# Pair-wide stacks, stores from GpSimd's queue and a scaling on ScalarE in a two-layer encoder on one NeuronCore

## The chip, the core and the metric

The kernel runs on one core of one Trainium2 chip. A core has five engines that run their own instruction streams: TensorE (PE, with its weight load shown apart as PEld), VectorE (DVE), ScalarE (ACT), GpSimd (POOL) and SyncE (SP, which here only issues DMAs). DMAs are issued by SP, ACT and POOL; the profile calls the issuing sides SPq, ACTq and POOLq. The metric is the device time of one execution in microseconds (us). A change of 0.5% is about 12 us.

## What is computed

The reference is a two-layer bidirectional encoder on a sequence of 512 tokens of width 1024, in float32. Each layer is a half-step SwiGLU feed-forward part, a mixer, and another half-step feed-forward part, each between two RMS norms. The change touches the mixer and the projection in front of it:

```python
u = rmsnorm(h, mix_pre_g[l])
proj = u @ w_in[l]
qa, ka, va, qb, kb, vb, qc, kc, vc, gl = jnp.split(proj, split_at, axis=-1)
oa = neighbourhood_attention(...)   # A: 8 heads of 64, 2-D window and bias
ob = sliding_window_attention(...)  # B: 8 query heads, 2 key heads, rotary, sink
# C: 4 heads, two maps each, rotary
sc = jnp.einsum('bhtqd,bhtkd->bhtqk', qblk, k).astype(jnp.float32) * (d ** -0.5)
p = jax.nn.softmax(sc, axis=-1)
a = p[:, :, 0] - lam * p[:, :, 1]
o = jnp.einsum('bhqk,bhke->bhqe', a.astype(v.dtype), v)
...
merged = jnp.sum(gates * yb, axis=2)   # yb: three branches through w_branch
h = h + rmsnorm(merged @ w_out[l], mix_post_g[l])
```

## The kernel before

Every matrix product is made from parts: a float32 value x is split into `hi`, a rounded copy that ACT writes, and `lo`, the rest x - hi, that DVE writes (`split`, lines 348 to 357). A dense product is then three matmuls, hi by hi, hi by lo and lo by hi (lines 326 to 328 for one output block, 680 in the projection's faster scheme). The weights are fetched in pieces of 512 KB (line 211) by SP or by ACT, and split by ACT (L224) and DVE (L225) on the way to PE.

For attention the parts are stacked instead. A head has 64 channels, so a tile of 128 partitions holds `hi` of a head in one half and `lo` in the other. A product of a stack of q with the stack of k sums hi by hi and lo by lo, a second one with the swapped stack of k (lo on top of hi) sums the cross terms. Each stack is filled by two DMAs, one for each half. The output channels of the projection come in blocks of 128, which are two heads: a *pair*.

*The projection* (profile time 350 to 508 us in the first layer, 1540 to 1707 in the second) makes all blocks of q, k, v. `stacked` (L1414) splits a block; those of pair 0 of branch A are stacked at once into the tiles `early`, all others are stored to memory as `part` by `store` (L1403, its DMA is L1405, issued by SP): `hi` and `lo` are separate regions there. `turned` transposes v and stores its two parts, or keeps them for pair 0. q and k of branch C are stored as they are, as `raw`.

*The mixer* (508 to 860, 1707 to 2060) runs a list of units, ORDER (line 72): `qa`, `qb`, `qc` bring in a pair or head, `aa`, `ab`, `ac` are the attentions, `ga` to `gc` are gate products, `ya` to `yc` the branches' products with w_branch. The list says in which order the work is written; a scheduler then places each engine's instructions, so that PE does gate and branch products (L326 to L328) between the pieces of attention. The units around the change:

- `restacked` (L1753) brings a pair's stacks back: for each head one stack of q, and for k the stack and the swapped stack. Each half is a DMA of SP (L1762, L1763, the tile `st`). With q of a pair and k of a pair these are 12 DMAs of 128 KB.
- `values` loads v's two parts, as two DMAs (`load`, L1739). The bias rows (L1712, `braw`) and the masks (L1706) are loads of SP as well.
- `softmax_pv` is the attention of A and B: products with k and swapped k (L1659), softmax, and in `rest` the transposes (L1690) and products with v (L1693, L1694).
- `attn_c` is the attention of branch C. For each of the four blocks of 128 queries of a head, and each of two maps: products (L1843, L1844), the maximum on DVE (L1845, L1846), the exponential on ACT (L1850). Then DVE takes the reciprocal of both sums (L1854), scales the second map by its reciprocal and by minus lambda (L1855), and adds the scaled first map (L1858). In `rest` PE transposes the result (L1867) and multiplies with v (L1870 to L1872); DVE copies the output out of PSUM (L1874), ACT squares it (L1877).
- `qkv_c` loads q and k of a head of branch C from `raw`, turns them by the rotary tables on DVE (L1748 to L1750), splits them and stacks them with DMAs between tiles (`stacks`, L1625).
- `combine` multiplies a branch, takes the gate (`gate`), which for branches B and C comes back from memory into the tiles `gd`, and adds to `merged` with GpSimd (L1916). At the end `merged` is split into M (L1970).

SP issues its DMAs in the order of its own list: an issue that waits holds all that stand behind it.

## Time and profile before

| | |
|---|---|
| median of three runs | 2406.46 us (2402.06 to 2411.33) |
| the profiled execution | 2405.37 us |
| its span on the core | 2403.6 us |
| mean granted clock of TensorE | 0.994 |

The span is the time from the first to the last instruction in the trace; 1.8 us of the execution's time lie around it. Busy times of matmuls are modelled ends in a pipeline, so rows of PE can overlap and be longer than the distance from one start to the next. "PE x <- DVE y" in a list of waits says that PE stood idle until an instruction of DVE, at the line named, had ended. The columns of a window's row are its limits, its length, the busy time and number of instructions of each engine, the clock that TensorE was granted (1 is full speed), the share of the 16 DMA engines that was busy, and GB/s.

### The profile page before, as it was taken

To read this page: it belongs to the slowest core of one execution; us is meant where nothing else is said; L and a number is where in the kernel's file an instruction comes from. 1 tells how busy PE (TensorE), PEld (TensorE's weight loads), DVE (VectorE), ACT (ScalarE), POOL (GpSimd) and SP (SyncE) were. 2 spreads that over 40 slices of the span, in tenths; PEclk is the share of its full clock that TensorE was granted. 3 is DMA by queue.
4 is the path that set the end of the run, shared out by engine and by line. 5 is a ranking of instruction groups with operands and counts; after the bars stand their busy time and mean duration, and the time that the engine had idled before them with its cause. 6 is when DMAs were issued, how large, how long until landed. Compare 5 with 4: busy or idle time off the path is not lost. (4 is left out here: it accounts for less than half of the span.)

```text
span 2403.6 us, 39852 instructions
## 1 busy us (share of the span) xinstructions
PE 2356.8 (98%) x15062; PEld 2109.1 (88%) x15062; DVE 1891.1 (79%) x3048; ACT 1425.7 (59%) x2671; POOL 156.5 (7%) x166
## 2 busy tenths in 40 slices
PE   9999999999999999999999999999899999999998
PEld 8999889988877789998899998899788777899987
DVE  7887978957987577888878878888489775788796
ACT  6565666658755365655655555666587553656563
POOL 0111000000001300110001100000000012011100
PEclk9999999999999999999999999999999999999999
DMA  5566535676565534655525565366765655246642
GB/s 168 159 172 188 161 137 189 202 207 199 162 189 160 162 112 132 173 159 166 178 88 158 167 176 184 118 209 200 209 190 150 195 163 158 97 144 171 190 145 89
DMA packets 149152, 395.13 MB, mean 164 GB/s; under 512 B 19296, under 2 KB 26080, under 8 KB 148448
## 3 DMA queue, kind: packets, MB, share of 16 engines
q1 hardware_dynamic: 127920, 303.38, 39.9%
q10 hardware_dynamic: 15408, 55.66, 7.5%
q0 software_dynamic: 5632, 33.56, 6.6%
q8 instruction: 118, 1.93, 0.3%
q14 instruction: 74, 0.61, 0.1%
HBM read 326.98 MB, written 80.74 MB: 170 GB/s over the span
## 5 line engine op out<-in xcount | busy, mean ns | idle before, releaser
L680 PE MATMUL mm<-X,h 128*128 128x256 f32 x1472 | 261.8, 278 | 0.7 <-DVE v L738 0.7
L225 DVE TENSOR_TENSOR w<-wr,w 128x512 fp32r<-128x512 f32 x272 | 189.3, 706 | 67.7 <-ACT w L224 64.0
L224 ACT ACTIVATE w<-wr 128x512 fp32r<-128x512 f32 x272 | 167.8, 627 | 113.0 <-PE mm L328 64.5
L326 PE MATMUL mm<-X,w 128*128 128x512 f32 (+1 forms) x602 | 229.6, 381 | 3.1 <-ACT X L553 1.8
L327 PE MATMUL mm<-X,w 128*128 128x512 f32 (+1 forms) x602 | 229.1, 380 | 0.8 <-DVE X L554 0.7
L328 PE MATMUL mm<-X,w 128*128 128x512 f32 (+1 forms) x602 | 229.6, 381 | 0.0
L680 PEld LDWEIGHTS mm<-X,h 128*128 128x128 f32 x1472 | 223.4, 188 | 2.0 <-DVE v L738 1.5
L680 PE MATMUL mm<-ht,l 128*128 128x256 f32 x736 | 205.8, 280 | 0.0
L680 PE MATMUL mm<-ht,h 128*128 128x256 f32 x736 | 205.6, 279 | 0.0
L680 PE MATMUL mm<-lt,h 128*128 128x256 f32 x736 | 204.9, 278 | 0.0
L680 PE MATMUL mm<-X,l 128*128 128x256 f32 x736 | 203.6, 277 | 0.0
L680 PE MATMUL mx<-lt,h 128*128 128x256 f32 x736 | 203.6, 277 | 0.0
L680 PE MATMUL mx<-ht,h 128*128 128x256 f32 x736 | 203.5, 277 | 0.0
L680 PE MATMUL mx<-ht,l 128*128 128x256 f32 x736 | 203.4, 276 | 0.0
L630 DVE TENSOR_TENSOR l<-wr,h 128x1024 fp32r<-128x1024 f32 x92 | 112.5, 1223 | 64.0 <-PE mm L680 64.0
L680 PE MATMUL at<-X,w 128*128 128x256 f32 x1104 | 141.2, 277 | 0.0
L662 ACT ACTIVATE h<-wr 128x1024 fp32r<-128x1024 f32 x92 | 97.7, 1062 | 73.2 <-PE mx L680 52.6
L680 PEld LDWEIGHTS mm<-ht,l 128*128 128x128 f32 x736 | 138.8, 189 | 0.0
L680 PEld LDWEIGHTS mm<-lt,h 128*128 128x128 f32 x736 | 138.7, 188 | 0.0
L680 PEld LDWEIGHTS mm<-ht,h 128*128 128x128 f32 x736 | 138.6, 188 | 0.1
L680 PEld LDWEIGHTS mx<-lt,h 128*128 128x128 f32 x736 | 138.3, 188 | 0.1
L680 PEld LDWEIGHTS mx<-ht,h 128*128 128x128 f32 x736 | 138.2, 188 | 0.1
(432 smaller groups left out, 6722.9 us busy)
## 6 DMA issues: line engine op xcount, KB each, us to landing
wr<-in_wts_dram SPq DMA_DIRECT2D x269, 512.0 KB
wr<-in_wts_dram ACTq DMA_DIRECT2D x106, 512.0 KB
sum<-in_wts_dram POOLq DMA_DIRECT2D x64, 512.0 KB, 5.1
st<-part SPq DMA_DIRECT2D x120, 128.0 KB
ap<-in_wts_dram SPq DMA_DIRECT2D x20, 512.0 KB
a<-kept SPq DMA_DIRECT2D x32, 256.0 KB
ap<-sum SPq DMA_DIRECT2D x16, 512.0 KB
x<-part SPq DMA_DIRECT2D x32, 256.0 KB
```

The lines of the kernel that those rows point to most:

```text
L224: A.activation(hi, raw, AF.Copy)
L225: V.tensor_tensor(out=lo, in0=raw, in1=f(hi), op=ALU.subtract)
L326: PE.matmul(acc, w[0], x[0], start=start, stop=False)
L327: PE.matmul(acc, w[0], x[1], start=False, stop=False)
L328: PE.matmul(acc, w[1], x[0], start=False, stop=stop)
L630: V.tensor_tensor(out=w["l1"], in0=self.raws[g][0], in1=f(w["h1"]), op=ALU.subtract)
L662: A.activation(self.W[g]["h24"], self.raws[g][1], AF.Copy)
L680: PE.matmul(acc, ws[i], xs[j], start=start and k == m == 0, stop=stop and k == n - 1 and m == 2, skip_group_check=True,)
```

## The change

- In `restacked` and in `stacks` a tile `st` now holds the same stack of both heads of a pair side by side (128 partitions by 2 by 512). The tag has 7 buffers of twice the size instead of 14. The tiles `early` of pair 0 are taken two slots at a time.
- `store` writes `hi` and `lo` of a block into one region of memory, one above the other, and its DMAs are issued by GpSimd's queue. One DMA of `restacked` then fills one half of a tile for both heads, so q and k of a pair are 6 DMAs of 256 KB. `values` is one DMA.
- In `attn_c` DVE multiplies the reciprocal of the second map (128 by 1) with minus lambda, and ACT scales the map. ACT copies the output from PSUM.
- The gates of branch C's combination come back into tiles of the tag `tx` (5 buffers), those of branch B stay in `gd` (2 buffers). M's tiles are doubles, too.

```diff
-        def store(kind, x):
-            d = dr.tile([P, T], F32, tag=kind, name=nm(kind), bufs=60)
-            nc.sync.dma_start(d, f(x))
+        def store(kind, *xs):
+            d = dr.tile([len(xs) * P, T], F32, tag=kind, name=nm(kind), bufs=60)
+            for n, x in enumerate(xs):
+                G.dma_start(d[n * P : n * P + P], f(x))
             return d
...
     def stacks(x, both):
         hi, lo = split(x, "tx")
         res = []
-        for s in range(2):
-            own = slice(64 * s, 64 * s + 64)
-            st = big("st", F32R, name="st")
-            nc.sync.dma_start(f(st)[0:64], f(hi)[own])
-            nc.sync.dma_start(f(st)[64:128], f(lo)[own])
...
+        for one, two in ((hi, lo), (lo, hi))[: 2 if both else 1]:
+            st = big("st", F32R, (P, 2, T), name="st")
+            for s in range(2):
+                own = slice(64 * s, 64 * s + 64)
+                nc.sync.dma_start(f(st)[0:64, s, :], f(one)[own])
+                nc.sync.dma_start(f(st)[64:128, s, :], f(two)[own])
+            res.append(st)
         return res
...
-            hi, lo = made[c]
             res = []
-            for s in range(2):
-                own, pair_ = slice(64 * s, 64 * s + 64), []
-                for one, two in ((hi, lo), (lo, hi))[: 2 if both else 1]:
-                    st = big("st", F32R, name="st")
-                    nc.sync.dma_start(f(st)[0:64], one[own])
-                    nc.sync.dma_start(f(st)[64:128], two[own])
-                    pair_.append(st)
-                res.append((pair_ + [None])[:2])
+            for order_ in (0, 1)[: 2 if both else 1]:
+                st = big("st", F32R, (P, 2, T), name="st")
+                for n in range(2):
+                    src = made[c][P * (n ^ order_) : P * (n ^ order_) + P].rearrange("(s q) t -> q s t", s=2)
+                    nc.sync.dma_start(f(st)[64 * n : 64 * n + 64], src)
+                res.append(st)
             return res
 
         def values(c):
-            t = made[c] if c == VA else [load(d, F32R, "st") for d in made[c]]
+            if c == VA:
+                t = made[c]
+            else:
+                t = big("st", F32R, (P, 2, T), name="v")
+                nc.sync.dma_start(f(t), made[c].rearrange("(n p) t -> p n t", n=2))
+            t = [t[:, n, :] for n in range(2)]
...
                 V.reciprocal(out=lc, in_=lc)
-                V.tensor_scalar(
-                    out=pm[1], in0=pm[1], scalar1=lc[:, 1:2], scalar2=nlam[:, l : l + 1], op0=ALU.mult, op1=ALU.mult
-                )
+                V.tensor_scalar(out=lc[:, 1:2], in0=lc[:, 1:2], scalar1=nlam[:, l : l + 1], scalar2=None, op0=ALU.mult)
+                A.activation(pm[1], pm[1], AF.Copy, scale=lc[:, 1:2])
...
-                V.tensor_copy(o, op)
+                A.activation(o, op, AF.Copy)
...
-                    t = load(t, tag="gd")
+                    t = load(t, tag="gd" if n == 1 else "tx")
```

On SP, at the start of the first layer's mixer, the loads of pair 1's stacks before (one row is one DMA; numbers tell tiles apart, `part` 4051 and 4053 are `hi` and `lo` of q, 4102 and 4104 those of k):

```order
L1762 DMA st_5805<-part_4051 64x512
L1763 DMA st_5805<-part_4053 64x512
L1762 DMA st_5808<-part_4051 64x512
L1763 DMA st_5808<-part_4053 64x512
L1762 DMA st_5811<-part_4102 64x512
L1763 DMA st_5811<-part_4104 64x512
L1762 DMA st_5814<-part_4104 64x512
L1763 DMA st_5814<-part_4102 64x512
L1762 DMA st_5817<-part_4102 64x512
L1763 DMA st_5817<-part_4104 64x512
L1762 DMA st_5820<-part_4104 64x512
L1763 DMA st_5820<-part_4102 64x512
```

The first four are q of the two heads; then come, for head 0 and then head 1, k and swapped k. The same place now, with v and the next pair's bias rows behind it (x2 is two DMAs, one for each half of the tile; lines after the change are up to four lower):

```order
L1758 DMA st_5786<-part_4051 64x2x512 x2
L1758 DMA st_5789<-part_4101 64x2x512 x2
L1758 DMA st_5792<-part_4101 64x2x512 x2
L1767 DMA v_5795<-part_4156 128x2x512
L1709 DMA braw_5974<-in_rpb_dram 128x1x512
L1709 DMA braw_5976<-in_rpb_dram 128x1x512
```

q, k and swapped k of both heads are three tiles; the swapped k of both heads come last, and v is one load.

On PE, the first products of pair 1 before. `st_5811` is the stack of k of head 0, `st_5814` the swapped one, `st_5805` q; `mm` rows are gate products:

```order
L1659 MATMUL mx_6039<-st_5811,st_5805 128x256
L1659 MATMUL mx_6043<-st_5811,st_5805 128x256
L326 MATMUL mm_6181<-X_3648,w_5988 128x512
L327 MATMUL mm_6181<-X_3649,w_5988 128x512
L328 MATMUL mm_6181<-X_3648,w_5988 128x512
L1693 MATMUL o_5896<-hi_5900,early_3957 128x2x128
L326 MATMUL mm_6181<-X_3648,w_5988 128x512
L327 MATMUL mm_6181<-X_3649,w_5988 128x512
L1694 MATMUL o_5896<-lo_5901,early_3957 128x2x128
L1690 MATMUL at_5924<-cons,s_5835 128x128 x2
L1659 MATMUL mx_6039<-st_5814,st_5805 128x256
L1659 MATMUL mx_6043<-st_5814,st_5805 128x256
```

Eight rows stand between the products with k and those with swapped k. Now the same stretch begins so, with `st_5789` for k and `st_5786` for q:

```order
L1656 MATMUL mx_5998<-st_5789,st_5786 128x256
L1656 MATMUL mx_6002<-st_5789,st_5786 128x256
L327 MATMUL mm_6340<-X_3647,w_6143 128x512
L328 MATMUL mm_6340<-X_3646,w_6143 128x512
L326 MATMUL mm_6340<-X_3646,w_6143 128x512
L327 MATMUL mm_6340<-X_3647,w_6143 128x512
L328 MATMUL mm_6340<-X_3646,w_6143 128x512
L1690 MATMUL o_5866<-hi_5879,early_3957 128x256
```

and ends, two weight products and one product with v later, with the swapped k, `st_5792`:

```order
L1687 MATMUL at_6025<-cons,s_5839 128x128 x2
L1690 MATMUL o_5866<-hi_5888,early_3957 128x256
L328 MATMUL mm_6340<-X_3646,w_6143 128x512
L326 MATMUL mm_6340<-X_3646,w_6143 128x512
L1691 MATMUL o_5866<-lo_5889,early_3957 128x256
L1690 MATMUL o_5866<-hi_5897,early_3957 128x256
L1656 MATMUL mx_5998<-st_5792,st_5786 128x256
L1656 MATMUL mx_6002<-st_5792,st_5786 128x256
```

Fifteen rows stand between the first products with k and those with swapped k: nine weight products, five products with v, and a row of two transposes.

On DVE, the end of a head of branch C's first blocks before, with the scaling of the second map at L1855 (`e`) and the sum at L1858 (`s`):

```order
L1854 RECIPROCAL lc_7760<-lc_7760 128x2
L1855 TENSOR_SCALAR e_7773<-e_7773,lc_7760,misc 128x512
L1845 TENSOR_REDUCE nm_7797<-mx_7798 128x1
L1858 SCALAR_TENSOR_TENSOR s_7759<-s_7759,lc_7760,e_7773 128x512
L1854 RECIPROCAL lc_7778<-lc_7778 128x2
L1846 TENSOR_SCALAR nm_7797<-nm_7797 128x1
```

Now on ACT, the same place: the scaling is L1855, the exponentials of the two maps are L1849 (`s` and `e`), `w` is a weight's cast and `wr` a weight fetch that ACT issues:

```order
L1849 ACTIVATE e_7691,lc_7678<-mx_7686,nm_7679 128x512
L1849 ACTIVATE e_7710,lc_7697<-mx_7705,nm_7698 128x512
L224 ACTIVATE w_7874<-wr_7872 128x512
L211 DMA wr_8142<-in_wts_dram 128x1024
L1855 ACTIVATE e_7691<-e_7691,lc_7678 128x512
L1855 ACTIVATE e_7710<-e_7710,lc_7697 128x512
L1849 ACTIVATE s_7677,lc_7716<-mx_7718,nm_7717 128x512
L1849 ACTIVATE e_7729,lc_7716<-mx_7724,nm_7717 128x512
L224 ACTIVATE w_8088<-wr_7872 128x512
L1855 ACTIVATE e_7729<-e_7729,lc_7716 128x512
```

On DVE the reciprocal and the sum stay, with a product of 128 by 1 between them; the scaling of 128 by 512 stands on ACT behind a cast, and in front of the next block's exponentials.

57 lines of the change are left out of this document (30 added, 27 removed).

## Prediction

> **What bounds the kernel now.** I read the page's first part, then the waits of PE, then windows over the stages that the change touches, then the timeline and the chain at the longest wait.
>
> ```profile
> span 2403.6 us, 39852 instructions
> PE 2356.8 (98%) x15062; PEld 2109.1 (88%) x15062; DVE 1891.1 (79%) x3048; ACT 1425.7 (59%) x2671; POOL 156.5 (7%) x166
> ```
>
> PE is busy for 2356.8 of 2403.6 us, so work saved on another engine counts only where PE waits for it, or where the waiting has made PE's clock slower. The waits of PE (engine, line, what it waited for: us in total, times, longest):
>
> ```profile
> PE mx L1659 <- DMA st<-part: 12.8, 4, 4.7
> PE mm L326 <- DVE x L1912: 8.2, 8, 2.0
> PE o L1871 <- DVE lo L353: 4.8, 2, 2.9
> ...
> PE at L1867 <- DVE s L1858: 2.0, 4, 0.6
> ```
>
> The longest is for stacks that come back from memory (L1762, L1763): a thing the diff edits. The third is in branch C. Windows place them; after the busy times stand the granted clock, the DMA share and GB/s:
>
> ```profile
> core 0: us, PE busy (x) PEld busy (x) DVE busy (x) ACT busy (x) POOL busy (x), PEclk, DMA share, GB/s
> 350.00:508.00 158.00, 157.26 (x1236) 151.08 (x1236) 126.89 (x174) 99.43 (x185) 0.00 (x0) 1.00 0.58 189
> 508.00:860.00 352.00, 337.74 (x1667) 275.23 (x1666) 258.60 (x632) 215.80 (x508) 25.50 (x16) 0.99 0.61 178
> 520.00:530.00 10.00, 6.12 (x35) 4.91 (x34) 6.05 (x26) 9.04 (x29) 0.00 (x0) 1.00 0.81 202
> 530.00:534.00 4.00, 4.00 (x15) 3.46 (x16) 0.00 (x0) 0.00 (x0) 0.00 (x0) 0.57 0.84 240
> 620.00:720.00 100.00, 97.36 (x482) 79.06 (x481) 87.15 (x207) 61.93 (x142) 0.00 (x0) 0.99 0.63 179
> 718.00:722.00 4.00, 4.00 (x14) 3.13 (x13) 3.05 (x7) 2.01 (x5) 0.00 (x0) 0.57 0.06 21
> 1707.00:2060.00 353.00, 336.22 (x1657) 274.62 (x1657) 261.19 (x637) 216.34 (x515) 25.53 (x16) 0.98 0.58 171
> 1732.00:1738.00 6.00, 4.43 (x16) 3.87 (x17) 0.00 (x0) 0.00 (x0) 0.00 (x0) 0.50 0.71 221
> 1906.00:1913.00 7.00, 6.36 (x17) 5.07 (x18) 5.18 (x9) 2.38 (x5) 0.00 (x0) 0.52 0.10 38
> ```
>
> In the projection (350 to 508) PE stands idle 0.7 us of 158. In the mixers (508 to 860 and 1707 to 2060) it is idle for 14.3 and 16.8 us, and after the long waits the clock falls: 4.0 us at 0.57 cost 4.0 x 0.43 = 1.7 us, 6.0 at 0.50 cost 3.0, and in branch C 1.7 and 7.0 x 0.48 = 3.4. With its clock the wait for stacks is worth 12.8 + 1.7 + 3.0 = 17.5 us, the one at L1871 4.8 + 1.7 + 3.4 = 9.9.
>
> Why the stacks are late is in the timelines of SP, ACT and PE around the first of the four (start, duration, engine, line):
>
> ```profile
> 520.54 0.45 SPq L1762 DMA_DIRECT2D st<-part  x1
> 526.09 0.45 SPq L1763 DMA_DIRECT2D st<-part  x1
> 516.77 0.34 ACTq L211 DMA_DIRECT2D wr<-in_wts_dram  x1
> 529.94 0.47 PE L1659 MATMUL mx<-st,st 128*128 128x256 f32 x2 [3.80 <-DMA st<-part]
> ```
>
> SP issues nothing from 520.99 to 526.09, between the two halves of one stack, though that load needs nothing of an engine. The chain of waits, at the same place of the second layer, tells what it stood for:
>
> ```profile
> 1704.13 8.86 DMA wr<-in_wts_dram
> 1713.00 2.70 DMA st<-part
> 1715.84 0.47 PE mx L1659 x2
> 1716.31 0.24 PE mm L326
> ...
> 1719.71 9.67 DMA wr<-in_wts_dram
> 1729.40 3.97 DMA st<-part
> ```
>
> A weight fetch that ACT issued takes 8.86 and 9.67 us, and only on its landing does the next half stack go out, which lands 2.70 to 3.97 us later. SP is held by a fetch that it didn't issue. By the order of the loads the row at 520.54 is the fifth of the pair's twelve half stacks; the sixth, behind the hole, is the second half of head 0's k, without which PE cannot start the pair.
>
> **The change part by part.** *The A and B stacks in fewer transfers.* A pair's twelve loads become six of twice the size, and the queries and k of both heads are the first four of them. If the same fetch holds SP at the same moment, what is caught is the last half of the swapped k stack. The order in the part on the change shows PE using that one later: between the first products with k and the first with swapped k stand nine 512-column weight matmuls, by the chain's row 9 x 0.24 = 2.2 us, and seven products with v or transposes at no more than that each, 1.7 at most; I take 3. PE came to the wait at 529.94 - 3.80 = 526.1 and would so need the swapped half at 529.1. It would land where the half of before did, 529.9, plus 128 KB more at the 202 GB/s of 520 to 530, 0.65 us: 530.6. A wait of at most 1.5 us stays of 3.8, or 6 over four places; where PE's longer queue before the pair covers more, none. I take 2.5 in all. The drops of the clock should go with the long waits; I count 4 of their 4.7 us. Together -(12.8 - 2.5) - 4 = **-14.3**, ends -17.5 (nothing stays) and -6.8 (6 us stay, and the clock's part too).
>
> On the clock: the drop at 718 (0.57) came after a wait of 1.90 us, in the row of L1871 that follows, so a stay of 1.5 us at a place is near what costs a drop, and I don't count the 4.7 in full. The Trainium skill ("TensorE: Matmul & The Clock Gate", section "HAM oscillation — how this bites in real kernels") puts the bound at idle gaps of more than about 3.4 us. The 1.90 us gap disagrees; by the page all 4.7 us would go and the term be -15.0.
>
> *Branch C.* The rows of DVE and PE show PE's wait at L1871: DVE stands at L1748 for q of the next head, and the `lo` that PE needs is queued behind it.
>
> ```profile
> 715.08 0.69 DVE L1748 TENSOR_TENSOR x<-x,cosR 128x512 f32<-128x512 f32 x1 [2.91 <-DMA x<-raw]
> 717.09 0.50 PE L1871 MATMUL o<-lo,x 128*128 128x512 f32 x1 [1.90 <-DVE lo L353]
> ```
>
> The load of q stands on SP behind the values. One values load instead of two saves about one issue, 0.45 us by SP's rows, at each of the two places, 0.9 us; if more of the queue runs ahead, up to the 9.9. The head-of-line arrangement on DVE is as it was, so I take **-3**; ends 0 and -9.9.
>
> *The second map's scaling and the copy of oc.* Rows by line and by group (min/median/max ns, or mean ns after the bar):
>
> ```profile
> L1855 DVE TENSOR_SCALAR e<-e,lc,misc x32: 533/543/548, 669.0 to 1960.9; 128x512 f32<-128x512 f32 x32
> L1846 DVE TENSOR_SCALAR nm<-nm x64: 131/146/154, 658.2 to 1958.9; 128x1 f32<-128x1 f32 x64
> L1874 DVE COPY oc<-o x8: 680/682/684, 687.3 to 1970.2; 128x512 f32<-128x512 f32 x8
> L1877 ACT ACTIVATE sqt<-o x8: 597/599/602, 688.0 to 1970.9; 128x512 f32<-128x512 f32 x8
> L224 ACT ACTIVATE w<-wr 128x512 fp32r<-128x512 f32 x272 | 167.8, 627 | 113.0 <-PE mm L328 64.5
> ```
>
> DVE loses 32 x 0.543 + 8 x 0.682 = 22.8 us and gains 32 x 0.146 = 4.7. ACT has no such row; by the cast of the same shape, 32 x 0.627 + 8 x 0.599 = 24.9 us more, half in each layer: 61.93 of the 100 us from 620 to 720 become 74, under PE's 97.36. As work it is hidden. As latency, each of 32 blocks gets 0.146 + 0.627 - 0.543 = 0.23 us longer, and the scale waits on ACT behind at most one other instruction of 0.63: 0.23 to 0.86. PE waits for L1858 in 4 blocks of 32 today; at those, 0.9 to 3.4 us. Against it a DVE that is 87% busy gets lighter, which can give back the 2.0 there. Behind a waiting scale on ACT stand the next exponentials and casts. I take **+1**; ends -2 and +3.4 here, and all 32 blocks are a rival.
>
> *Stores by GpSimd.* In the projection they leave SP's queue, and weight fetches no longer stand behind a store that waits for `lo`; PE's idle time there is 0.7 us of 158, so **-0.5** over two layers, at most -1.5. At the mixer's start the masks wait for the last stores:
>
> ```profile
> L277 POOL DMA_DIRECT2D sum<-in_wts_dram x32 | 16.2, 507 | 0.0
> sum<-in_wts_dram POOLq DMA_DIRECT2D x64, 512.0 KB, 5.1
> 510.19 1.83 SPq L1405 DMA_DIRECT2D part<-lo  x1
> 512.08 1.34 SPq L1706 DMA_DIRECT2D mask<-in_tables_dram  x2
> ```
>
> The masks go out 1.9 us after the last store; by GpSimd a store costs 0.51 us to issue by the nearest row and, by its only row of landings, up to 5.1 to land, so masks, biases and stacks may start up to 4 us later in each layer. The nearest row is twice the size and from HBM, so I take 1 us each, **+2**; ends 0 and +8. GpSimd has room: 46 stores a layer at 0.51 us are 23 of 158 us.
>
> *Gate loads of branch C's combination in other buffers; the merged rows in double tiles.* The wait for L1912 ends with an addition on GpSimd and a split after it, both untouched: **0**, ends -2 and 0.
>
> Sum: -14.3 - 3 + 1 - 0.5 + 2 = -14.8, on the profiled execution's 2405.4 us 2390.6; the median of the three runs lies 1.1 us above that execution, so **2391**.
>
> **The rivals.** *1. The stage is full of transfers, and the wait only moves.* For it: DMA share 0.81 to 0.84 at the holes, the same bytes as before, the fetch that holds SP untouched. Against it: PE needs the held piece later. If the long transfers share the engines with the fetch and all land as late as the swapped half, each place keeps 2.6 of its 3.2 us and the drops: the term is -2, the sum -2.5, 2404. The Trainium skill says so of queues ("DMA: Bandwidth & Descriptors", section "Issuing engines are not separate DMA queues"): DMAs of all issuers interleave on the same 16 engines, and another issuer saves issue time alone.
>
> *2. Slower: the scale on ACT ends PE's cover.* In branch C each block's transposes (L1867) wait for L1858, now after a hop to ACT. If all 32 pay 0.86 us, that is 27.5 us; with the other terms, -15.8 + 27.5 = +11.7: 2418. It overtakes the gain from 18 blocks on. For it: ACT works in order, with casts in front of the scale. Against it: PE waits at 4 blocks today, for 2.0 us, and ACT is 62% busy.
>
> *3. The stores by GpSimd land late.* With the full +8 and a clock drop at each of the two starts (1.7 each by the row at 530), +11.4 stand in place of +2: -5.4, 2401.
>
> **How the numbers follow.** 0.5% is 12 us, about what a measurement of this kernel can tell from no change. The forecast's case has 0.62; near its weak end (-7) it stays within 12, which I give 0.08 of these. Rival 1 has 0.22 and rival 3 0.07, both within 0.5%; rival 2 has 0.09. Faster 0.54, same 0.37, slower 0.09. The forecast's ends, not all at once, make 2378 (A whole, C's 9.9 half) to 2404; rivals 1 and 3 lie inside, and up to 2410 half of rival 2's way is covered, so the range is 2378 to 2410.
>
> **What would show it.** Right: PE's wait for stacks at 3 us or less, no granted clock under 1 near 530 and 1735, and SP's hole still there, between other loads. Wrong: a new wait at the products with swapped k of 2 us or more; a longer row for L1867 on the scale; masks that go out after 515; or a wait at L1871 that has grown, since DVE still stands in front of a load.

## The result and the profile after

The change made the kernel slower: 2421.71 us (median of 5 runs, 2417.27 to 2425.49) beside 2404.56 (5 runs, 2402.06 to 2411.33), a ratio of 1.0070 with a 95% interval of 1.0054 to 1.0085. The forecast was 2391. The profiled execution took 2425.49 us, its span is 20.1 us longer than that of before, and the mean granted clock is 0.993.

The page's first part, after:

```profile
span 2423.7 us, 39845 instructions
PE 2357.8 (97%) x15062; PEld 2107.9 (87%) x15062; DVE 1879.2 (78%) x3040; ACT 1448.4 (60%) x2711; POOL 207.0 (9%) x258
```

PE's work is what it was (2356.8 before); DVE lost 11.9 us and ACT gained 22.7. So nearly all of the 20 us is time in which PE stands idle. The waits of PE (us in total, times, longest) say for what:

```profile
PE mx L1656 <- DMA st<-part: 21.7, 6, 6.4
PE mx L1656 <- DVE nmx L1659: 8.1, 5, 2.6
PE mm L326 <- DVE x L1910: 3.9, 7, 0.7
PE mx L1842 <- ACT s L1849: 3.9, 2, 2.5
PE o L1869 <- DVE lo L353: 3.3, 3, 1.5
...
PE at L1865 <- DVE s L1856: 0.6, 1, 0.6
```

The wait for stacks, which the change was expected to shorten from 12.8 to 2.5 us, is 21.7. Behind it stands a new one, for the maxima of attention (`nmx`), which DVE makes from the products and the bias. Branch C's waits did get shorter: L1869 is L1871 of before (4.8), L1865 is L1867 (2.0).

Not all of this is stacks. Early in the mixer DVE itself stands for bias rows (L1709):

```profile
519.00 0.43 DVE L1720 TENSOR_TENSOR bedge<-braw,mask 128x256 f32<-128x256 f32 x1 [2.63 <-DMA braw<-in_rpb_dram]
523.06 0.43 DVE L1720 TENSOR_TENSOR bedge<-braw,mask 128x256 f32<-128x256 f32 x1 [2.21 <-DMA braw<-in_rpb_dram]
```

Behind these PE stands 2.20 us up to 520.57, counted under `nmx`, and 1.89 us up to 523.89. The second is counted under `st`, but the product it holds is one of pair 0, whose stacks don't come from memory, and it starts right behind DVE's maximum (523.75 to 523.84); so it belongs to the bias rows. The other long wait for maxima in this layer, 2.63 us up to 584.14, is another thing: the maxima stand on DVE behind the split of a weight whose fetch landed at 582.4.

Windows of the same stretches place the loss (busy time and count of each engine, granted clock, DMA share, GB/s). First before, where the rows of the second layer and of the first mixer's start have not been shown; then after:

```profile
508.00:640.00 132.00, 125.85 (x682) 105.77 (x681) 99.10 (x310) 98.28 (x269) 0.00 (x0) 0.99 0.68 190
640.00:760.00 120.00, 116.91 (x561) 94.05 (x559) 101.61 (x224) 71.92 (x154) 5.01 (x3) 0.99 0.65 187
1707.00:1840.00 133.00, 125.03 (x686) 105.89 (x686) 104.54 (x333) 101.47 (x287) 0.00 (x0) 0.97 0.63 182
```

```profile
350.00:508.00 158.00, 156.82 (x1227) 150.45 (x1227) 126.10 (x172) 99.99 (x185) 23.52 (x44) 1.00 0.61 193
508.00:640.00 132.00, 115.25 (x617) 97.18 (x616) 89.45 (x287) 92.52 (x256) 1.35 (x3) 0.95 0.67 164
640.00:760.00 120.00, 115.28 (x557) 92.68 (x557) 93.35 (x214) 75.01 (x157) 3.34 (x2) 1.00 0.65 189
1707.00:1840.00 133.00, 117.69 (x630) 98.72 (x629) 92.39 (x294) 94.16 (x260) 2.07 (x4) 0.96 0.69 167
```

The projection (350 to 508) is as before, 156.8 us of PE against 157.3. In the first part of each mixer, where A and B's stacks come in, PE does 125.85 - 115.25 = 10.6 and 125.03 - 117.69 = 7.3 us less than before: 17.9 of the 20.1. From 640 to 760, in branch C, it is 1.6. And in the bad stretch the 16 DMA engines are as busy as before (0.67, 0.68) but move 164 GB/s where they moved 190.

The timeline after, at the first pair that comes back from memory, and at the worst waits of the two layers:

```profile
513.70 2.98 SPq L1709 DMA_DIRECT2D braw<-in_rpb_dram  x4
516.77 9.31 SPq L1758 DMA_DIRECT2D st<-part  x6
...
530.64 2.98 SPq L1709 DMA_DIRECT2D braw<-in_rpb_dram  x2
533.82 14.62 SPq L1758 DMA_DIRECT2D st<-part  x6
```

```profile
534.71 0.47 PE L1656 MATMUL mx<-st,st 128*128 128x256 f32 x2 [2.81 <-DMA st<-part]
553.24 0.55 PE L1656 MATMUL mx<-st,st 128*128 128x256 f32 x1 [5.89 <-DMA st<-part]
1733.25 0.55 PE L1656 MATMUL mx<-st,st 128*128 128x256 f32 x1 [6.37 <-DMA st<-part]
```

SP issues the first stack at 516.77, about as before (516.4). PE gets it at 534.71, 18 us later. What happened in those 18 us stands in the completion events of the trace. This table is made from them: the issue of a load (us), its landing (the last of its events), and which of eight semaphores it counts on.

```
                before                     after
4 bias rows     513.5 -> 518.5  s105       513.7 -> 518.9  s108
                514.3 -> 520.5  s106       514.6 -> 523.0  s109
                515.1 -> 523.8  s109       515.3 -> 527.6  s100
                515.7 -> 527.3  s110       516.0 -> 530.6  s101
ACT's weights   516.8 -> 526.1  s108       515.0 -> 525.5  s110
stacks          516.4 -> 527.6  s100       516.8 -> 531.7  s104
                517.2 -> 528.0             517.5 -> 532.9  s105
                518.0 -> 528.4             518.2 -> 533.8  s106
                518.6 -> 528.9             518.9 -> 534.6  s108  PE starts
                520.5 -> 529.4  s106       523.1 -> 535.4  s109
                526.1 -> 529.8  s108       525.5 -> 536.3  s110
                  ^ PE starts
                six more, to 532.5
```

Three things stand here. First, no stack lands before the fourth bias row has, 527.3 before and 530.6 after: a stack that went out at 516.4, ahead of the hole on SP, landed 11.2 us later, behind the bias rows. Second, the bias rows themselves land one after another, 2.0 to 3.4 us apart before and 3.0 to 4.6 after the change. Third, by the single events, only half of a stack was held up. A bias row has one event about 1.1 us after its issue and eight at its end (525.7 to 527.3 for the fourth before, 529.4 to 530.6 after). The first stack behind them has eight early, at 522.7 to 522.9 before and 522.5 to 523.1 after, and eight late, at 526.3 to 527.6 and 530.7 to 531.7. PE needs all sixteen.

### The profile page after: what moved, and what is told of

The parts are those of the page before. It is cut to its first block, busy times and chain, and to the rows that moved or that the text cites. A ratio compares the mean times of both kernels' runs of the same rounds, so it can differ in the third digit from the quotient of the medians.

```text
span 2423.7 us, 39845 instructions
## 1 busy us (share of the span) xinstructions
PE 2357.8 (97%) x15062; PEld 2107.9 (87%) x15062; DVE 1879.2 (78%) x3040; ACT 1448.4 (60%) x2711; POOL 207.0 (9%) x258
```

## The experiments

The first four runs do one part alone each: the stores, the scaling, and the order of the loads.

**Stores by GpSimd alone** (before, with this edit):

```diff
-            nc.sync.dma_start(d, f(x))
+            G.dma_start(d, f(x))
```

> The kernel before with one edit: the stores of the projection are issued by GpSimd instead of SP. Theory 'late start' (the mixer's masks, bias rows and stacks wait for GpSimd's stores and start 2 to 3 us later in each layer): 4 to 8 us slower than before, 2409 to 2413 us, with the masks' issue 2 us or more later against the last lo of the projection. Theory 'pair-wide loads' (PE's first product of a pair needs q and k of both heads, behind the bias rows in one queue): no loads are changed here, so within 3 us of before, 2402 to 2408. Theory 'hop to ACT' expects no change either.

2406.68 us beside 2407.25; ratio 0.9993 (0.9982 to 1.0004). The store's queue costs nothing.

**The whole change with its stores back on SP:**

```diff
-                G.dma_start(d[n * P : n * P + P], f(x))
+                nc.sync.dma_start(d[n * P : n * P + P], f(x))
```

> The kernel after with one edit: the stores go back to SP. Theory 'pair-wide loads': the loss stays, 2415 to 2422 us, and PE's wait for the stacks stays above 16 us in total. Theory 'late start': most of the loss goes, 2404 to 2411. Theory 'hop to ACT': unchanged, 2419 to 2424.

2424.18 beside 2407.25; ratio 1.0064 (1.0047 to 1.0081). The loss stays, and the two runs agree on the time. The wait for stacks was expected above 16 us and is 10.8:

```profile
PE mx L1656 <- DMA st<-part: 10.8, 3, 5.6
```

So the total of this one row doesn't follow the loss: PE stands elsewhere in its place, 7.1 us for maxima and 6.5 for branch C's sums.

**The scaling and the copy on ACT alone** (before, with the change's lines in `attn_c`):

> The kernel before with branch C's edits alone: the second map's scaling and the copy of the output from PSUM on ACT, the reciprocal times minus lambda on DVE. Theory 'hop to ACT': 6 us or more slower than before, 2411 or more, by waits of PE at the transposes and products of branch C. Theories 'late start' and 'pair-wide loads': within 4 us of before, 2401 to 2409.

2407.79 beside 2407.25; ratio 1.0000 (0.9990 to 1.0011). It costs nothing and gains nothing.

**The change with its stacks loaded head by head** (the same double tiles, but twelve loads of 128 KB in the order of before):

```diff
...
+            for s in range(2):
+                for order_, st in enumerate(res):
+                    for n in range(2):
+                        r = P * (n ^ order_) + 64 * s
+                        nc.sync.dma_start(f(st)[64 * n : 64 * n + 64, s, :], made[c][r : r + 64])
```

> The kernel after with one edit: the stacks come back head by head in twelve DMAs of 128 KB for a pair, q, k and swapped k of head 0 first, into the same double tiles and from the same regions; stores stay on GpSimd. Theory 'pair-wide loads': most of the loss goes, 2403 to 2411 us, since head 0 needs three quarters of a MB less in front of its first product. Theory 'late start': it stays, 2416 to 2423. Theory 'hop to ACT': unchanged, 2419 to 2424.

2414.44 beside 2407.25; ratio 1.0026 (1.0015 to 1.0037). About 60% of the loss is gone. (By the order of the loads PE needs 0.75 MB in front of its first product, as before the change, and 1 MB with loads of a pair: 0.25 MB less, not the three quarters that were expected.) Its waits, and the window from the first bias row on, where the next two rows are before and after:

```profile
PE mx L1656 <- DVE nmx L1659: 8.8, 6, 3.5
PE mx L1656 <- DMA st<-part: 7.3, 3, 3.0
```

```profile
513.00:548.00 35.00, 28.77 (x146) 23.54 (x144) 18.49 (x67) 21.58 (x62) 0.00 (x0) 0.95 0.78 188
```

```profile
513.00:548.00 35.00, 29.47 (x150) 24.44 (x149) 18.38 (x67) 21.57 (x63) 0.00 (x0) 0.95 0.80 201
```

```profile
513.00:548.00 35.00, 27.45 (x140) 22.50 (x138) 18.57 (x66) 20.75 (x60) 0.00 (x0) 0.95 0.89 177
```

With loads by head the DMA engines are busy for 0.78 and the wait for stacks is 7.3 us; with loads of a pair they are busy for 0.89 and move less. In the trace's packets the median one of 2 KB on SP's queue takes 84 ns before, 91 here and 167 after, in the same 35 us.

**Who is to blame: the tiles, the loads, or the bias rows?** The next four: the whole change but the double tiles; loads by head in branch C too; and the bias rows taken off SP's queue, in both kernels.

```diff
-            nc.sync.dma_start(raw, bass.AP(rpb.tensor, ...
+            G.dma_start(raw, bass.AP(rpb.tensor, ...
```

> The kernel before with all of the change but the double tiles: stores by GpSimd into one region for hi and lo, the second map's scaling and the copy on ACT, branch C's gates in tx; the stacks are single tiles of one head again, 14 of them, filled and read as before, and v is two loads. Theory that all of the loss lies in the double tiles and their loads: 2403 to 2409. Rival 'sum of small things' (stores, region, scaling and gates together): 2411 or more.

2402.25 beside 2403.44; ratio 0.9993 (0.9982 to 1.0005). Everything in the change but the pair-wide tiles, with one region and one store for a block, costs nothing. The loss lies in the double tiles and how they are loaded.

> The kernel after with two edits: the stacks of branches A and B come back head by head in 128 KB transfers, and those of branch C are filled map by map (stack and swapped stack of the first map first, as before the change). The first edit alone gave 2414. Theory 'order of branch C's stacks' (the rest of the loss is the swapped stack of the first map coming third): back to before, 2404 to 2410. Rival 'double tiles' (the rest is that a double buffer is released only when both heads are done with): it stays at 2411 to 2417.

2408.62 beside 2403.44; ratio 1.0021 (1.0008 to 1.0034). Against the 1.0026 of loads by head in A and B alone this is no difference that the intervals allow. That what is left of the loss, 5 to 6 us, comes from branch C's stacks is not shown.

> The kernel after with one edit: the bias rows (braw) are issued by GpSimd, the stacks stay on SP. Theory 'behind the bias rows' (the stacks land only when the four bias rows that SP issued ahead of them have landed, since one queue is served in order): the stacks land within 6 us of their issue, PE's wait for them falls under 8 us from 21.7, and the time falls by 10 us or more, to 2400 to 2412. Rival 'full engines' (the bytes set the landing, whatever the queue): the wait stays above 14 us and the time at 2417 to 2424.

2422.14 beside 2403.44; ratio 1.0076 (1.0056 to 1.0096). The time stays, though the wait for stacks goes:

```profile
PE mx L1656 <- DVE nmx L1659: 10.3, 8, 4.1
PE o L1691 <- DVE lo L353: 6.6, 4, 2.1
PE mx L1656 <- DMA st<-part: 4.3, 4, 2.5
```

The longest of them, on DVE and then on PE:

```profile
521.59 0.42 DVE L1720 TENSOR_TENSOR bedge<-braw,mask 128x256 f32<-128x256 f32 x1 [4.36 <-DMA braw<-in_rpb_dram]
```

```profile
523.15 0.58 PE L1656 MATMUL mx<-early 128*128 128x256 f32 x1 [4.14 <-DVE nmx L1659]
```

PE has the four stacks of pair 1 at 529.2 in place of 534.6, but now the bias rows are late: DVE stands 4.36 us for the first of them, which lands at 521.6 (518.9 with the change as it is), and PE for DVE's maxima. The wait for stacks fell as the theory said, the time did not. Which queue the loads stand in decided which of the two came late; the DMA engines are busy for 0.98 of these 35 us, and packets on SP's queue still take 154 ns.

> The kernel before with the same edit: the bias rows by GpSimd, all else as it was. Theory 'behind the bias rows': PE's wait for stacks falls from 12.8 to under 5 us and the time by 8 us or more with the clock that goes with it, to 2391 to 2399. Rival 'full engines': 2403 to 2410, no change.

2398.22 beside 2403.44; ratio 0.9983 (0.9971 to 0.9995). In the kernel before the same edit gains a little, less than the 8 us that the theory asked for; the interval stops just short of no change. The wait for stacks is 4.9 us, as expected.

**Why are the loads of a pair slow?** One theory was that a load of both heads takes its rows alternately from two places in memory 64 rows apart; the next run stores the heads' rows next to each other (by twice as many stores), so that a load reads pieces of 4 KB:

```diff
...
-                    src = made[c][P * (n ^ order_) : ...].rearrange("(s q) t -> q s t", s=2)
+                    src = made[c][P * (n ^ order_) : ...].rearrange("(q s) t -> q s t", s=2)
```

> The kernel after with one edit: in memory the rows of the two heads of a pair stand side by side (row 2q + s for channel q of head s), written by two stores of GpSimd for each part; the loads keep their number and size, 256 KB, but read 4 KB in a piece where they read 2 KB from two places 128 KB apart. In the kernels with long loads the median packet of 2 KB on SP's queue takes 135 to 167 ns at the mixer's start, in those with loads of 128 KB of one head 84 to 113. Theory 'alternating rows' (it is the jump between the two heads' rows that slows the packets): the bytes flow as before, the stacks of pair 1 have landed by 533 instead of 536 us, and the time falls by 8 us or more, to 2405 to 2413. Rival 'size' (a long transfer in front delays all behind it, and PE needs both heads at once): the time stays at 2416 to 2424.

2425.36 beside 2407.54; ratio 1.0075 (1.0062 to 1.0089). The theory falls: the median packet of 4 KB takes 307 ns, nearly as long as two of 2 KB (168 each in this run), the time is what it was, and PE's wait is long still:

```profile
PE mx L1661 <- DMA st<-part: 17.5, 4, 6.8
```

The counterpart keeps the alternating rows but makes the loads as short as those of before:

```diff
-                    nc.sync.dma_start(f(st)[64 * n : 64 * n + 64], src)
+                    for h in (0, 32):
+                        nc.sync.dma_start(f(st)[64 * n + h : 64 * n + h + 32], src[h : h + 32])
```

> The kernel after with one edit: each load of 256 KB is two of 128 KB, of 32 channels of both heads each, so that the loads are as short as before the change but still read from two places 128 KB apart. Theory 'alternating rows': the median 2 KB packet on SP's queue stays at 135 ns or more at the mixer's start, the DMA engines stay near 0.9 busy at about 180 to 205 GB/s, and the time stays at 2415 or more. Rival 'size': packets of 84 to 113 ns and a time of 2405 to 2413, as with the loads of one head.

2444.87 beside 2407.54; ratio 1.0161 (1.0145 to 1.0176). As a time this tells little of loads: with them the scheduler moved attention later in PE's order (the first product with a stack from memory comes 32 matmuls later in PE's trace, at 539.12 in place of 534.71 us, and PE doesn't wait for it). Its packets say more: 115 ns at the median, between 84 and 167, with the rows still alternating.

Long loads of one head, 256 KB each, with the double tiles as they are (hi and lo of a head stored one above the other):

```diff
...
+                own = made[c][P * s : P * s + P]
+                nc.sync.dma_start(f(res[0])[:, s, :], own)
...
```

> The kernel after with one edit: the stores put hi and lo of each head one above the other, so that a stack of one head is one load of 256 KB of 128 whole rows, and the swapped one two of 128 KB; 8 loads for a pair, head 0's q, k and swapped k first, into the same double tiles. Theory 'size' (a load of 256 KB is slower for its bytes than one of 128): packets of 135 ns or more on SP's queue at the mixer's start, and 2414 to 2424. Rival 'pair' (only the bundling of two heads costs, by what PE must wait for): packets of 84 to 113 ns and 2405 to 2413, as with twelve loads by head.

2409.80 beside 2408.38; ratio 1.0001 (0.9990 to 1.0013). So neither the length of a load nor the double tile must cost anything; PE needs 0.75 MB here in front of its first product, and packets take 104 ns. Most of the loss comes from loads that carry two heads.

```profile
PE mx L1660 <- DMA st<-part: 5.5, 4, 2.2
```

**The bias rows made plain.** A bias load reads 128 rows of 2 KB that overlap in memory, and in the trace it completes with 9 events where other loads have 16. In both kernels it is replaced by a load of the same size from plain rows, which leaves out the true bias:

```diff
-            nc.sync.dma_start(raw, bass.AP(rpb.tensor, (l * 8 + hd) * 16 * RPBW, [[RPBW, 8], ...
+            nc.sync.dma_start(raw, tables[:, 0:512])
```

> The kernel after with one edit: each bias row load (256 KB from 128 overlapping rows that start 4 or 256 bytes apart, in which only 9 of 16 completions show) is a plain load of the same size from the tables, so the bias is not the reference's. Theory 'long loads hold up the bias rows' (the half of the DMA engines that carry the bias rows share the memory with the other half, on which the long stacks run ahead, and the stacks land only behind the bias rows): the loss against the kernel before with the same edit shrinks from 17 us to under 6, and PE's wait for stacks falls under 8 us from 21.7. Rival 'long loads themselves' (a pair's first product needs 1 MB in place of 0.75, whatever runs in front): the loss stays above 10 us.

> The kernel before with the same edit of the bias rows, as the other half of the comparison (the bias is not the reference's). Theory 'long loads hold up the bias rows': PE's wait for stacks falls from 12.8 us to under 5, and the time by 8 us or more against before. Rival 'long loads themselves': it falls by less than 5 us here, since the wait is for the weight fetch that holds SP.

On the same chip, beside 2408.38 us of the kernel before: 2399.30 with the change, ratio 0.9959 (0.9946 to 0.9971), and 2400.00 without it, ratio 0.9956 (0.9941 to 0.9972). Beside each other the two don't differ, so the change's loss is gone, within the intervals of some 0.15% each. PE's wait for stacks is 3.8 us with the change and 4.9 without, both under the bounds of the theory. The windows at the mixer's start, with the change and then without it:

```profile
508.00:640.00 132.00, 123.44 (x674) 104.09 (x672) 98.32 (x304) 97.11 (x265) 2.14 (x4) 0.99 0.67 180
513.00:548.00 35.00, 30.14 (x159) 25.19 (x158) 19.53 (x69) 22.84 (x66) 0.00 (x0) 0.97 0.93 238
```

```profile
508.00:640.00 132.00, 127.53 (x694) 107.64 (x693) 101.58 (x318) 99.25 (x273) 0.00 (x0) 0.99 0.66 195
513.00:548.00 35.00, 31.14 (x163) 26.11 (x162) 19.05 (x68) 22.41 (x65) 0.00 (x0) 0.95 0.82 240
```

The same 35 us that moved 177 GB/s after the change now move 238, on engines that are about as busy (0.93, 0.89). In the landing table the fourth bias row comes at 525.5 (530.6 after the change) and at 519.8 (527.3 before), and the stacks begin right behind it in both, at 526.0 and 520.4. Packets take 125 ns with the change and 84 without, so loads of two heads are slower by themselves; and from 508 to 640 PE still does 4.1 us less than without the change, which later stretches make up (2.7 of it from 1840 to 1960).

**Can the gains be had together?** The single tiles with the bias rows issued by GpSimd:

> The change without its double tiles (stores by GpSimd into one region, scaling and copy on ACT, branch C's gates in tx, single tiles and 128 KB loads as before) and with the bias rows issued by GpSimd, the one edit that gained on the kernel before (ratio 0.998). Theory 'the gains add': 2393 to 2400 us where before is at 2404. Rival 'GpSimd holds the bias rows behind its stores': 2401 to 2408.

2412.43 beside 2408.38; ratio 1.0011 (1.0000 to 1.0023). They don't add up: beside 2404, as the forecast has it, this ratio makes 2407, in the rival's range. GpSimd issues the first bias row at 515.8, after its last store at 510.1, and it lands at 524.3; with single tiles alone SP issued it at 512.7 and it landed at 517.7. PE waits early for the maxima:

```profile
PE mx L1663 <- DVE nmx L1666: 9.2, 2, 6.4
```

**Plain rows with the reference's result.** The bias rows are copied into a plain region of memory by GpSimd's queue ahead of the mixer, which then loads plain rows. First with the copies paced by the projection's outputs, in the kernel before, in the change, and in the change with single tiles:

```diff
+        def spread_out(hd):
+            d = spreadb[l, hd] = dr.tile([P, T], F32, tag="bias", name=nm("bias"), bufs=16)
+            G.dma_start(d.rearrange("(a b) t -> b a t", b=16), bass.AP(rpb.tensor, ...))
...
+                paced([lambda hd=unspread.pop(0): spread_out(hd)], x[:, 0:1])
...
-            nc.sync.dma_start(raw, bass.AP(rpb.tensor, ...
+            nc.sync.dma_start(raw, spreadb[l, hd])
```

> The kernel before with one edit that keeps its result: GpSimd copies each head's 128 overlapping bias rows within memory into a plain region of 256 KB during the projection, and the mixer loads them from there in whole rows. Theory 'the bias rows' form' (they move on half of the DMA engines and everything behind them in SP's queue waits): as in the run with plain rows, 2396 to 2402 us where before is at 2405, with the stacks of pair 1 landed by 531 us. Rival 'the copies cost what the rows gain' (8 copies a layer, 2 MB read and 2 MB written in the projection, where the DMA share is 0.58): 2403 to 2409.

> The kernel after with the same edit. Theory 'the bias rows' form': the loss of the change goes, 2396 to 2404 us, and PE's wait for stacks falls under 8 us from 21.7. Rival 'long loads themselves': above 2412.

> The change without its double tiles (single tiles and 128 KB loads as before the change, all else of it kept) with the same edit of the bias rows. If the pieces add, 2394 to 2401 us, the best of the three; if the long loads are an advantage once the bias rows are plain, 2 us or more behind the kernel after with the same edit.

Beside 2403.12: before with copies 2401.43, ratio 1.0004 (0.9990 to 1.0019); the change with copies 2408.44, ratio 1.0026 (1.0012 to 1.0040); single tiles with copies 2405.16, ratio 1.0005 (0.9993 to 1.0016). The change's wait for stacks falls to 3.7 us and its loss by some 11 us, but the projection pays: from 350 to 508 PE is busy for 150.8 us, 156.8 with the change as it is. The longest wait there (4.46 us up to 388.84) is behind ACT, and ACT stood for a weight fetch of SP, which took 9.5 us beside the copies (377.65 to 387.16) and 6.0 with the change as it is (376.88 to 382.91). The other layer has the same wait at 1579.3.

```profile
PE at L1442 <- ACT x L1408: 13.9, 8, 4.5
...
PE mx L1668 <- DMA st<-part: 3.7, 2, 3.5
```

```profile
387.19 1.06 ACT L625 ACTIVATE h<-wr 128x1024 fp32r<-128x1024 f32 x1 [6.44 <-DMA wr<-in_wts_dram]
```

Then with the copies made earlier, in the first feed-forward part, behind the weight sums that GpSimd loads there, in the kernel before:

```diff
...
+        if which == 1:
+            for hd in range(8):
+                n = len(steps) - 8 + hd
+                steps[n] = lambda step=steps[n], hd=hd: (step(), spread_out(l, hd))
```

> The kernel before with one edit that keeps its result: the bias rows of a layer are copied into plain regions of memory during its first feed-forward part, one behind each of eight weight sums that GpSimd issues there every 10 us, and the mixer loads them in whole rows. Theory 'the bias rows' form' (in the run that copied them in the projection the mixer gained and the projection lost the same): with the copies out of the projection, as in the run with plain rows, 2396 to 2402 us where before is at 2405, ratio 0.994 to 0.998. Rival 'copies cost wherever they are': 2403 or more.

2396.85 beside 2408.53; ratio 0.9957 (0.9942 to 0.9972). This is the fastest kernel with the reference's result, and as fast as the 0.9956 of plain rows that need no copies. The change was not run with these copies.

```profile
508.00:640.00 132.00, 127.86 (x697) 108.33 (x696) 101.89 (x322) 99.78 (x276) 0.00 (x0) 0.99 0.66 197
513.00:548.00 35.00, 31.41 (x164) 26.60 (x163) 18.96 (x69) 23.34 (x68) 0.00 (x0) 0.95 0.85 250
1707.00:1840.00 133.00, 129.33 (x702) 109.36 (x701) 108.29 (x335) 102.93 (x288) 0.00 (x0) 0.97 0.62 181
```

In the two stretches PE gets 127.86 - 125.85 = 2.0 and 129.33 - 125.03 = 4.3 us more done than in the kernel before.

## Why the prediction was wrong

The sum of the terms comes to 2391.7, and 2391 was put down; nothing hangs on it.

**The stacks, -14.3: wrong in sign, and the step that failed is the landing.** The prediction read the hole on SP (nothing issued from 520.99 to 526.09) as the cause, and wrote that the swapped half "would land where the half of before did, 529.9, plus 128 KB more at the 202 GB/s of 520 to 530, 0.65 us: 530.6". After the change it landed at 536.3, and what PE starts with, which was to be early since it went out ahead of the hole, at 534.6. In place of the -14.3 stand 8.9 us more of waiting for stacks (12.8 to 21.7, of which 1.9 belong to the bias rows), and more time at the low clock. The hole is real and was rightly put to ACT's weight fetch: in the table the sixth stack counts on the same semaphore as that fetch, and goes out as it lands (526.1 and 526.1 before, 525.5 and 525.5 after). But it was not what set the end. The stacks ahead of the hole were no earlier, because they stood in one queue behind four bias rows: half of their completions came only behind those of the fourth. The prediction counted when loads are issued; what PE waits for is when they land, and for that every load ahead of them in the queue counts.

Three things made the landing late; no run gives each its price. The bias rows landed later, the fourth by 3.3 us (530.6 against 527.3). Behind it PE needed four stacks of 256 KB, 1 MB, the last of them 4.0 us after the fourth bias row; before, it needed six of 128 KB, 0.75 MB, and they came 2.5 us after. And what lands late holds its semaphore: the bias rows of the next pair went out at 530.6 and 533.0, as the fourth bias row and the second stack landed, and landed at 542.2 and 545.2 (537.3 and 539.6 before). That is how the wait grows from 2.81 us at 534.71 to 5.89 at 553.24, one of the prediction's "four places", at each of which a wait was to shrink. Its bound of -6.8 for the term was no bound, since it let the waits only shrink.

**The drops of the clock, 4 us of the term: not saved.** The first mixer's start falls from 0.99 to 0.95. By the trace's clock records the low clock is 0.50. In the first parts of the two mixers it lasts 10.2 us before (from 530.4 and 1731.9 on) and 23.9 after (from 523.3, 550.6, 584.8, 1731.6 and 1752.1). By the prediction's way of counting that is 5.1 us before and 11.9 after, an estimate and an upper one, since PE isn't busy throughout. Windows after the change:

```profile
518.00:523.00 5.00, 1.80 (x9) 0.96 (x7) 1.85 (x8) 2.03 (x6) 0.00 (x0) 1.00 1.03 207
523.00:527.00 4.00, 3.11 (x10) 2.68 (x11) 3.30 (x14) 2.56 (x9) 0.00 (x0) 0.57 1.05 181
...
550.00:558.00 8.00, 4.76 (x18) 4.21 (x19) 1.54 (x3) 2.04 (x5) 0.00 (x0) 0.57 1.06 206
```

The drop at 523 comes in a stretch in which PE worked 1.80 of 5 us. It begins at 523.32, inside the second of two waits in PE's timeline:

```profile
520.57 0.39 PE L1656 MATMUL mx<-early 128*128 128x256 f32 x1 [2.20 <-DVE nmx L1659]
523.89 0.58 PE L1656 MATMUL mx<-early 128*128 128x256 f32 x1 [1.89 <-DMA st<-part]
```

So short waits close together came with a lower clock, as a single one of 1.90 us did before. The Trainium skill ("TensorE: Matmul & The Clock Gate", section "HAM oscillation — how this bites in real kernels") puts the bound at gaps of more than about 3.4 us; these waits are shorter, and the measurement decides. What fits the two traces is a share of work. Every drop lasts 3.41 or 6.83 us, and in the 3.41 us in front of its start PE was busy for 0.00 to 0.44 of the time (1.43 us, 0.42, at 523.32). Of the stretches of 3.41 us in step with the drops after which the clock stayed full, the emptiest held 0.51 in either kernel (the first 100 and last 30 us left out). So the bound lay near half here; it is a rough one, for in other runs one drop followed 0.63 (the short alternating loads) and none followed 0.44 (single tiles with GpSimd's bias rows).

**Branch C, -3: the wait shrank, not shown why, and nothing in the time.** The wait behind `lo` (L1869) is 3.3 us, 4.8 before. The term had the load of q come sooner; DVE in fact stands longer for rotary loads, 14.2 us in all, 8.5 before. PE's busy time from 640 to 760 is 1.6 us less than before, with a wait of 3.9 us for ACT's exponentials (L1842) that was 0.7 before. How much of that is branch C's own, and how much comes from the late start, was not told apart.

**The gate loads, 0: the wait fell, which was not foreseen.** The wait behind the addition (L1910, before L1912) is 3.9 us, 8.2 before, more than the -2 that the term allowed at its end. It is 8.9 with single tiles and all else of the change, so the gates' other buffers don't bring it by themselves; what does is open.

**The scaling, +1: about right, measured 0.0 (-2.4 to +2.6).** The operations, after:

```profile
L1856 DVE SCALAR_TENSOR_TENSOR s<-s,lc,e 128x512 f32<-128x512 f32 x32 | 23.5, 746 | 2.6 <-ACT e L1855 2.3
L1855 ACT ACTIVATE e<-e,lc 128x512 f32<-128x512 f32 x32 | 23.1, 722 | 19.7 <-DVE lc L1854 10.2 <-DVE nm L1845 6.9 <-DVE lc L1853 2.3
```

The scale took 722 ns where the cast's 627 was taken; DVE waited 2.3 us for it in 32 blocks. The rival in which all 32 blocks pay fell with the run of the scaling alone.

**The stores, -0.5 and +2: measured -1.7 (-4.3 to +1.0).** The last store went out 1.4 us earlier than before, at 508.81. The last mask went out 4.4 us behind it, 2.9 before, so there was some of the delay that was feared; but the first bias row went out at 513.70, 0.2 us later than before, and the rival of late stores fell too.

```profile
508.81 0.54 POOL L1406 DMA_DIRECT2D part<-lo  x1
```

**The other rivals.** Nearest came "a stage full of transfers", which put the wait elsewhere and the time at 2404. It named the right resource, but took the engines' rate as given, and so had no way to a loss. The case that happened, packets that get slower with loads of two heads, was not among the rivals.

**What is still open.** With plain bias rows the change is free, and with loads by head it costs 0.26% or nothing, so most of the loss needs both the overlapping bias rows and loads that carry two heads. Why the two together slow the packets is not settled. Loads of two heads alone bring them from 84 ns to 125, with the bias rows to 167, and with these on another queue to 154. Alternating rows and the length of a load are not enough to explain it. Nor is it settled how much of the loss is late bias rows, how much slow packets, and how much the 0.25 MB more that PE needs for its first product. The remaining 5 to 6 us of loads by head are not explained either: in that run PE does 5.1 us less from 640 to 760 than before, and stands 3.52 us up to 644.75, while DVE stands 3.98 us at a rotary product whose load went out 7.6 us later than before (635.69 in place of 628.06). The long loads by head don't show this. And each edit made the scheduler order PE's work anew, which limits every comparison here to what the windows and landings show.

## What to carry to other kernels

Before loads are bundled, look at when they land, not when they are issued, and at what stands ahead of them in the same queue: a hole in the issuing engine's list can be real and still not be what sets the end. Count what the consumer must have before its first product; a bundle that brings two heads makes the first head wait for the second. A load of an odd form in front of a queue (here rows that overlap) is worth making plain in a stage that has time for it, which here made the kernel before 0.43% (0.28 to 0.58) faster.

## What the runs showed of the hardware

- On SP's queue a load of 128 overlapping rows of 2 KB completed with 9 events where plain loads have 16 (on GpSimd's it had 16), and held up half of what stood behind it: four of them took from 513.5 to 527.3 us before, and four plain loads of the same size from 512.6 to 519.8. The Trainium skill ("DMA: Bandwidth & Descriptors", section "Why a DMA increments its semaphore by 16 and not by 1") says that a transfer is split over the largest number of engines, up to 16, that divides the slowest dimension of both its sides. The bias rows' slowest dimension is 8, so by the page 8 engines would carry them. The trace agrees, with eight events at the end of such a load and eight late ones of each stack behind it, though no run shows which engine moved what.
- In this program the DMAs of SP and of ACT took eight completion semaphores in turn, and an issue waited until the load eight before it in the program's order had landed: 520.54 behind a bias row that landed at 520.52 (s106), 526.1 behind ACT's weights (s108). One slow load so holds the issue of the eighth after it, whatever that is and whoever issued it.
- GpSimd's issue of a store took 0.54 us and SP's 0.32, and the last stores landed 4.8 us after their issue on GpSimd's queue and 4.7 on SP's: no difference by queue.
- The median packet of 2 KB on SP's queue took 84 ns with loads of one head of 128 KB before the change, 104 with 256 KB of one head, 125 with 256 KB of two heads and plain bias rows, and 167 with the overlapping ones in front (all from 513 to 548 us).
